# Joining small TensorE steps of a hybrid attention and scan layer: the sample chunk, the outputs of two query blocks, and the form of the first logits

## The chip, the cores and the metric

The kernel runs on one core of a Trainium2 chip. The metric is the device time in microseconds; of several runs the median counts. Time before: 1369.97 us, median of 3 runs (1369.65 to 1371.65).

## What is computed

One layer of a streaming encoder for two request groups that share the weights: a prompt of 512 tokens and a sample of 32 tokens. From the reference, cut to what matters here:

```python
h = rmsnorm(x, g_mix)
q, k, v, z, xbc, dt_raw, gates = split(h @ w_in)
# A: attention; 16 heads of 64; the prompt is causal in chunks of 64 over its 512 tokens,
#    the sample attends to 256 cached rows and its own 32
logits = einsum('bihd,bjhd->bhij', q, k) * HEAD_DIM_A ** -0.5
ya = einsum('bhij,bjhd->bihd', softmax(logits + bias), v)
# B: Mamba-2 scan; 4 groups of 8 heads, chunked over the tokens
y = einsum('bijg,bijgr,bjgrp->bigrp', cb, decay, dx)
y = y + einsum('bign,bgrpn->bigrp', cc, hc) * exp(acs)[..., None]
h_new = hc * exp(last)[..., None, None] + einsum('bjgn,bjgrp->bgrpn', bc, wj)
x = x + (gate_a * (ya @ w_proj_a) + gate_b * (yb @ w_proj_b)) @ w_out
x = x + (gelu(ug) * uv) @ w_down          # ug, uv: causal convolution of rmsnorm(x) @ w_up
x = x + sigmoid(rmsnorm(x) @ w_ple_gate) * (p @ w_ple)
```

## The kernel before

Activations lie with features on partitions and all 544 tokens (512 of the prompt, 32 of the sample) on the free axis. Every dense product is cut into steps of 128 output features, and a step into chunks of 128 input features. A chunk (`Dense.chunk`, L310) is six matmuls `dps` (`mm3`, L273): weight and activation are split into a high and a low fp32r part, three products of them are summed, each for two halves of 272 tokens. One flat list of steps (`dense_steps`, L38) gives the order, and `dense.run(n)` issues the next n chunks. Each weight block is split by ACT (`wh`, L250) and by DVE or POOL (`wl`, L254) ahead of its step.

The scan and the attention are written by hand between those chunks, so that dense matmuls fill the time in which DVE, ACT and POOL prepare the next small matmuls. The order on TensorE is fixed as the program issues it (`Ordered`, L122): every matmul hangs on the one before. The order on the other engines and on SP, which issues the DMAs, is planned by the framework from a simulated timeline.

**Scan** (L1133 to L1147). 20 steps, four groups of 8 heads by five chunks: the sample (`c == 4`, 32 tokens), then prompt chunks 0 to 3 of 128. `ssd_a` (L613) makes the operands of a chunk: `cbt` and `xst` on TensorE, `dx`, `wj` and `bt`, and for each half of 4 heads a tile `ab` (a DMA that broadcasts a row to all partitions) and a tile `m` (Relu head by head, Exp, a mask). `ssd_b` (L661) comes one step later: for each pair of heads the matmuls `yps` from `m` and `dx`, then, in chunks with a state before them, `yps` from `ab` and the state `h`; DVE adds four slices of the result to `xs` (L682); a matmul `st` makes the new state. A step runs 7 chunks between `ssd_a` and `ssd_b` of the chunk before, and 6 behind it: 65 a group. The tiles `dx`, `wj`, `ab`, `m` share 14 buffers (`half_tile`, L607), `bt` has 2, the PSUM tiles of all small matmuls share 4 (`sps`, L172).

**Attention** (L1149 to L1174). Eight pairs of heads, each with four query blocks of 128 (`i` = 0 to 3); pairs with an even number begin with a block for the sample of two pairs (`i` = -1). For a block, `att_a` (L828) makes the logits `L` of both heads and their softmax `P`; one block later `att_b` (L862) transposes `P` (`Tp`) and ACT copies it to `PT`; after some chunks `att_c` (L884) multiplies with the values into `O`, and ACT copies `O` to `att`. `FILL` (L1149) says how many chunks stand before `att_b` and before `att_c`. Blocks 1 to 3 use a stacked form of fp32r operands, made by `stack` (L811) for each head (`hi`) of a pair: `ks` is the high part of k, which a DMA copies to the other 64 partitions; `qs` holds the high part of q on 64 partitions and its low part on the others, for tokens 128 to 511; `klz` is the low part of k. Block 0 takes `q` and `k` as they are, on 64 partitions, in fp32. `stack(m + 1, 0)` is called behind block 3's logits of pair m, `stack(m, 1)` behind block 0's. Each of these tiles has one buffer per head.

A matmul of fp32 operands appears as two instructions in the trace, one of fp32r as one.

Of the kernel before, what the change touches and what calls it, by code (L numbers as in the profile page):

```python
# [9 lines left out]
F32 = mybir.dt.float32  # L10
# [6 lines left out]
SEQ = 512  # L17
SMP = 32
# [98 lines left out]
def trunk(ctx: ExitStack, tc: tile.TileContext, a):  # L117
# [495 lines left out]
    def ssd_a(g, c):  # L613
# [26 lines left out]
        sts = [(bt[:Q], wj.rearrange("p a b -> p (a b)")[:Q])]  # L640
        ms, cps = [], []
        for hh in range(2):
            ab = half_tile("ab")
            src = asc[c, 8 * g + 4 * hh : 8 * g + 4 * hh + 4, 0:Q]
            nc.sync.dma_start(ab[:, :, :Q], src.unsqueeze(0).to_broadcast([128, 4, Q]))
            m = half_tile("m")
            for i in range(4):
                hd = 8 * g + 4 * hh + i
                S.activation(m[:Q, i, :Q], ab[:Q, i, :Q], AF.Relu, scale=-1.0, bias=tm[:Q, 1, c, hd : hd + 1])  # L649
            S.activation(m[:Q, :, :Q], m[:Q, :, :Q], AF.Exp, scale=-1.0)  # L650
            V.tensor_tensor(m[:Q, :, :Q], m[:Q, :, :Q],
                            cbm[:Q, :Q].unsqueeze(1).to_broadcast([Q, 4, Q]), op=MUL)
            ms.append(m)
            if inter:
                S.activation(ab[:, :, :Q], ab[:, :, :Q], AF.Exp)  # L655
                G.tensor_tensor(ab[:, :, :Q], ab[:, :, :Q],  # L656
                                cc[:, tk].unsqueeze(1).to_broadcast([128, 4, Q]), op=MUL)
                cps.append(ab)
        return dxf, sts, ms, cps

    def ssd_b(g, c, dxf, sts, ms, cps):  # L661
        q0 = 128 * c
        Q = 128 if c < 4 else SMP
        tk = slice(q0, q0 + Q)
        inter = c != 0
        hst = state[g, "s"] if c == 4 else state.get(g)
        yp = sps("yps")
        for pr in range(4):
            for hi in range(2):
                hd = 2 * pr + hi  # L670
                PE.matmul(yp[64 * hi : 64 * hi + 64, 128 * pr : 128 * pr + Q],
                          lhsT=dxf[:Q, 64 * hd : 64 * hd + 64], rhs=ms[hd // 4][:Q, hd % 4, :Q],
                          start=True, stop=not inter)
            if inter:
                for hi in range(2):
                    hd = 2 * pr + hi
                    PE.matmul(yp[64 * hi : 64 * hi + 64, 128 * pr : 128 * pr + Q],
                              lhsT=hst[:, 64 * hd : 64 * hd + 64], rhs=cps[hd // 4][:, hd % 4, :Q],
                              start=False, stop=True)
        for i in range(4):  # L680
            t = xs[4 * g + i]
            V.scalar_tensor_tensor(t[:, tk], t[:, tk], vec[:, V_DSK + 4 * g + i : V_DSK + 4 * g + i + 1],  # L682
                                   yp[:, 128 * i : 128 * i + Q], op0=MUL, op1=ADD)
        st = sps("st")
        for n, (l, r) in enumerate(sts):
            PE.matmul(st, lhsT=l, rhs=r, start=True, stop=True)
        hn = spt([128, 512], "h", 4)
        if inter:
            G.tensor_tensor(hn.rearrange("p (h f) -> p h f", f=64), hst.rearrange("p (h f) -> p h f", f=64),
                            el[:, c, 8 * g : 8 * g + 8].unsqueeze(2).to_broadcast([128, 8, 64]), op=MUL)  # L690
            V.tensor_tensor(hn, hn, st, op=ADD)
        else:
            S.copy(hn, st)
        if c == 4:
            nc.sync.dma_start(a["o_hs"][:, 512 * g : 512 * g + 512], hn)
        else:
            state[g] = hn
            ssd_done.add((g, c))
            if c == 3:
                nc.sync.dma_start(a["o_hp"][:, 512 * g : 512 * g + 512], hn)  # L700
# [110 lines left out]
    def stack(m, hi):  # L811
        q, k = qk["q", m], qk["k", m]

        def st(n, tag):
            return pools["ap"].tile([128, n], F32R, tag=tag, name=tag, bufs=1)

        kl = klz[hi]
        a0, b0 = 64 * hi, 64 - 64 * hi
        own, oth = slice(a0, a0 + 64), slice(b0, b0 + 64)
        qs, ks = st(384, f"qs{hi}"), st(512, f"ks{hi}")  # L820
        S.copy(ks[own], k[own, 0:512])
        nc.sync.dma_start(ks[oth].bitcast(F32), ks[own].bitcast(F32))
        S.copy(qs[own], q[own, 128:512])
        V.tensor_tensor(qs[oth], q[own, 128:512], qs[own].bitcast(F32), op=SUB)  # L824
        G.tensor_tensor(kl[own], k[own, 0:512], ks[own].bitcast(F32), op=SUB)
        stk[hi] = qs, ks, kl

    def att_a(m, i):  # L828
# [15 lines left out]
        for hi in range(2):  # L844
            p0 = 64 * hi
            L = sps("L")
            own = slice(p0, p0 + 64)
            if i == 0:
                PE.matmul(L[:, :n], lhsT=q[own, 0:n], rhs=k[own, 0:n], start=True, stop=True)
            else:  # L850
                qs, ks, kl = stk[hi]
                sl = slice(n - 256, n - 128)
                PE.matmul(L[:, :n], lhsT=qs[:, sl], rhs=ks[:, 0:n], start=True, stop=False)
                PE.matmul(L[:, :n], lhsT=qs[:, sl], rhs=kl[:, 0:n], start=False, stop=True)
# [7 lines left out]
    def att_b(m, i, Ps):  # L862
# [12 lines left out]
        for hi in range(2):  # L875
# [3 lines left out]
            pt = apt([128, 512], "PT", 2)  # L879
# [4 lines left out]
    def att_c(m, i, pts):  # L884
        O = sps("O")
        if i < 0:
            pt = pts[0]
            for w in range(2):
                cv, vs = qk["cv", m + w], qk["s", m + w]
                for j in range(3):  # L890
                    for hi in range(2):
                        p0 = 64 * hi
                        lhs = cv[:, j, p0 : p0 + 64] if j < 2 else vs[:, p0 : p0 + 64]
                        kk = 128 if j < 2 else SMP
                        o = 128 * j + 64 * w + 32 * hi
                        PE.matmul(O[p0 : p0 + 64, SMP * w : SMP * w + SMP], lhsT=lhs, rhs=pt[:kk, o : o + 32],
                                  start=j == 0, stop=j == 2)
            for w in range(2):
                if m + w not in att:
                    att[m + w] = slot(name="at", src=at_slots)  # L900
                S.copy(att[m + w][:, SEQ:T], O[:, SMP * w : SMP * w + SMP])
            return
        at, vt = att[m], qk["v", m]
        n = 128 * (i + 1)
        for j in range(i + 1):
            for hi in range(2):
                p0 = 64 * hi
                PE.matmul(O[p0 : p0 + 64, 0:128], lhsT=vt[:, 128 * j + p0 : 128 * j + p0 + 64],
                          rhs=pts[hi][:, 128 * j : 128 * j + 128], start=j == 0, stop=j == i)
        S.copy(at[:, 128 * i : n], O[:, 0:128])  # L910
# [235 lines left out]
    ssd_b(*prev)  # L1146
# [123 lines left out]
```

## Time and profile before

| | before |
|---|---|
| median of 3 runs | 1369.97 us |
| the profiled execution, time | 1369.19 us |
| its span | 1367.5 us |
| TensorE busy (matmuls) | 99% |
| DVE, ACT, POOL busy | 62%, 47%, 23% |

The span is what the profile covers; the time of the same execution has 1.7 us around it. A busy share of TensorE is not its pace: matmuls overlap in the records, so a matmul's length in a row is longer than its share of the time, and the pace is the distance between the starts of successive rows. In a timeline row the first number is the start, the second the length of the merged row, then engine, line, operation, output <- inputs, the tile shape of the array that the matmul uses (rows \* columns), the moving operand's shape, and xN for N instructions in the row.

### The profile page before, as it was taken

To read this page: it belongs to the slowest core of one execution; us is meant where nothing else is said; L and a number is where in the kernel's file an instruction comes from. 1 tells how busy PE (TensorE), PEld (TensorE's weight loads), DVE (VectorE), ACT (ScalarE), POOL (GpSimd) and SP (SyncE) were. 2 spreads that over 40 slices of the span, in tenths; PEclk is the share of its full clock that TensorE was granted. 3 is DMA by queue.
4 is the path that set the end of the run, shared out by engine and by line. 5 is a ranking of instruction groups with operands and counts; after the bars stand their busy time and mean duration, and the time that the engine had idled before them with its cause. 6 is when DMAs were issued, how large, how long until landed. Compare 5 with 4: busy or idle time off the path is not lost.

```text
span 1367.5 us, 26629 instructions
## 1 busy us (share of the span) xinstructions
PE 1350.5 (99%) x11045; PEld 1311.3 (96%) x11045; DVE 848.5 (62%) x1474; ACT 643.3 (47%) x1156; POOL 318.2 (23%) x446
## 2 busy tenths in 40 slices
PE   7999999999999999999999999999999999999998
PEld 6999999999899999999999999999999999999998
DVE  7998878855676555752545335677777447753545
ACT  5456565656576666652433223444444224431342
POOL 5446364543331111200000000033333013310000
PEclk9999999999999999999999999999999999999999
DMA  5733232433434323212222332222222232222231
GB/s 180 249 105 105 101 119 96 137 99 127 151 100 135 116 88 103 70 63 93 93 93 82 129 104 93 93 93 81 78 91 93 93 110 81 77 95 93 93 104 55
DMA packets 41961, 142.16 MB, mean 104 GB/s; under 512 B 9280, under 2 KB 13296, under 8 KB 29552
## 3 DMA queue, kind: packets, MB, share of 16 engines
q1 hardware_dynamic: 41840, 140.46, 30.9%
q8 instruction: 87, 1.43, 0.4%
q14 instruction: 34, 0.28, 0.1%
HBM read 129.27 MB, written 14.31 MB: 105 GB/s over the span
## 4 chain that ended last, share of the span: by engine, by line
PE 96%; DVE 1%; ACT 1%; DMA 0%; issue 0%; SPq 0%; DVEq 0%; ACTq 0%
PE dps L130 84%; PE yps L130 3%; PE O L130 2%; PE L L130 2%; PE st L130 2%; PE Tp L133 1%; PE xst L133 1%; DVE qs L824 1%; PE qn L130 0%; PE gps L130 0%; DMA xin<-in_xT 0%; PE cbt L130 0%; PE vt L133 0%; ACT wh L250 0%; ACT P L777 0%
## 5 line engine op out<-in xcount | busy, mean ns | idle before, releaser
L130 PE MATMUL dps<-hi,wh 128*128 128x272 f32 x2960 | 629.0, 294 | 1.2 <-ACT hi L374 0.5
L130 PE MATMUL dps<-lo,wh 128*128 128x272 f32 x2960 | 614.1, 289 | 5.6 <-DVE lo L375 5.6
L130 PE MATMUL dps<-hi,wl 128*128 128x272 f32 x2960 | 613.2, 289 | 0.0
L130 PEld LDWEIGHTS dps<-hi,wh 128*128 128x128 f32 x2960 | 466.9, 189 | 15.6 <-issue 10.9
L130 PEld LDWEIGHTS dps<-lo,wh 128*128 128x128 f32 x2960 | 466.8, 189 | 6.6 <-DVE lo L375 6.6
L130 PEld LDWEIGHTS dps<-hi,wl 128*128 128x128 f32 x2960 | 466.3, 189 | 0.0
L250 ACT CAST wh<-wr 128x1024 fp32r<-128x1024 f32 x192 | 201.4, 1049 | 395.3 <-PE dps L130 355.9
L254 DVE TENSOR_TENSOR wl<-wr,wh 128x1024 fp32r<-128x1024 f32 x173 | 214.6, 1240 | 49.2 <-ACT wh L250 43.8
L1026 DVE SCALAR_TENSOR_TENSOR ucv<-uext,vec,ucv 128x546 f32<-128x546 f32 x96 | 75.3, 785 | 4.1 <-ACT ucv L1023 2.4
L599 DVE SCALAR_TENSOR_TENSOR cv<-ext,hv,cv 128x547 f32<-128x547 f32 x72 | 68.7, 954 | 5.8 <-ACT cv L596 5.0
L1019 POOL COPY cfo<-uext 128x2 f32<-128x2 f32 x48 | 10.4, 217 | 260.4 <-DVE uext L573 260.4
L1016 POOL MEMSET uext<- 128x2 f32 x48 | 4.5, 94 | 278.3 <-issue 278.3
L1058 DVE TENSOR_TENSOR x<-x,dps 128x544 f32<-128x544 f32 x24 | 17.3, 721 | 78.0 <-PE dps L130 78.0
L254 POOL TENSOR_TENSOR wl<-wr,wh 128x1024 fp32r<-128x1024 f32 x19 | 47.5, 2500 | 58.4 <-ACT wh L250 58.4
L571 DVE TENSOR_TENSOR uext<-dps,rstd 128x272 f32<-128x272 f32 x48 | 21.2, 441 | 63.7 <-PE dps L130 59.0
L775 DVE CUSTOM_DVE_ANT_0 P<-L,bias 128x128 f32<-128x128 f32 (+3 forms) x64 | 30.9, 482 | 46.8 <-PE L L130 46.8
L1020 POOL COPY cfo<-uext 128x2 f32<-128x2 f32 x48 | 56.4, 1175 | 0.0
L649 ACT ACTIVATE m<-ab,tm 128x128 f32<-128x128 f32 (+1 forms) x160 | 48.3, 374 | 4.9 <-DMA ab<-asc 4.9
L777 ACT ACTIVATE P<-P,sm 128x128 f32<-128x128 f32 (+3 forms) x64 | 35.9, 561 | 23.7 <-DVE sm L775 23.5
L656 POOL TENSOR_TENSOR ab<-ab,bc 128x512 f32<-128x512 f32 (+1 forms) x32 | 40.2, 1262 | 28.7 <-ACT ab L655 28.6
L368 ACT CAST hi<-me 128x544 fp32r<-128x544 f32 x24 | 15.5, 647 | 61.9 <-DVE me L1044 61.9
L731 POOL TENSOR_TENSOR ql<-qs,qh 128x544 fp32r<-128x544 f32 x16 | 22.5, 1405 | 94.3 <-ACT qh L730 81.5
(240 smaller groups left out, 1564.5 us busy)
## 6 DMA issues: line engine op xcount, KB each, us to landing
wr<-in_w SPq DMA_DIRECT2D x96, 1024.0 KB, 4.9
ab<-asc SPq DMA_DIRECT2D x32, 256.0 KB, 5.1
bsc<-evec SPq DMA_DIRECT2D x16, 320.0 KB, 7.5
bias<-bsc SPq DMA_DIRECT2D x16, 256.0 KB, 3.6
xin<-in_xT SPq DMA_DIRECT2D x8, 272.0 KB, 5.1
out_o_v<-v SPq DMA_DIRECT2D x8, 272.0 KB, 2.5
out_o_k<-qk SPq DMA_DIRECT2D x8, 272.0 KB, 2.1
x<-in_xT SPq DMA_DIRECT2D x8, 272.0 KB, 4.4
```

The lines of the kernel that those rows point to most:

```text
L130: return self._pin(nc.tensor.matmul(*args, **kw))
L133: return self._pin(nc.tensor.transpose(*args, **kw))
L250: cp = S.copy(hi, r)
L254: eng.tensor_tensor(lo, r, hi.bitcast(F32), op=SUB)
L599: V.scalar_tensor_tensor(y[:, :n], ext[:, j : j + n], hv[:, 24 * j + ti : 24 * j + ti + 1], y[:, :n], op0=MUL, op1=ADD)
L649: S.activation(m[:Q, i, :Q], ab[:Q, i, :Q], AF.Relu, scale=-1.0, bias=tm[:Q, 1, c, hd : hd + 1])
L656: G.tensor_tensor(ab[:, :, :Q], ab[:, :, :Q], cc[:, tk].unsqueeze(1).to_broadcast([128, 4, Q]), op=MUL)
L731: G.tensor_tensor(lo[:, :T], sq[:, :T], hi[:, :T].bitcast(F32), op=SUB)
L775: V.tensor_tensor_reduce(out=P, in0=L, in1=B, scale=1.0, scalar=3e38, op0=ADD, op1=MIN, accum_out=nm[:n])
L777: S.activation(P, P, AF.Exp, scale=-1.0, bias=nm[:n], accum_out=sm[:n])
L1020: G.tensor_copy(cfo[:, i, 2:4], ext[:, UW - 2 : UW])
L1026: V.scalar_tensor_tensor(y[:, :n], ext[:, j : j + n], vec[:, V_FW + 48 * j + i : V_FW + 48 * j + i + 1], y[:, :n], op0=MUL, op1=ADD)
```

## The change

Four things are rearranged. (1) The sample chunk of a group has no step of its own: `ssd_a` for it and for chunk 0 stand together, and `ssd_b` takes both as one list: all `yps` of the sample (16 instructions from `m` and `dx`, then 16 from `ab` and `h`), then chunk 0's, then DVE's additions, then both `st`. The sample's eight heads lie in one `ab` and one `m`, with one DMA, one subtraction on DVE and one Relu on ACT in place of eight. 16 steps remain, with 65 chunks a group as before. (2) `att_c` takes two blocks at one place (0 and 1 with the sample, if there is one; 2 and 3), with one `O` and one copy for both. (3) Block 0 uses the stacked form too: `qs` covers all 512 tokens, and both heads are stacked behind block 3's logits of the pair before. (4) `PT` of even blocks has two buffers of its own.

```diff
@@ ssd_a
-        for hh in range(2):
-            ab = half_tile("ab")
-            src = asc[c, 8 * g + 4 * hh : 8 * g + 4 * hh + 4, 0:Q]
-            nc.sync.dma_start(ab[:, :, :Q], src.unsqueeze(0).to_broadcast([128, 4, Q]))
...
+        H = 4 if c < 4 else 8
+        for h0 in range(0, 8, H):
+            ab = half_tile("ab").rearrange("p a b -> p (a b)")[:, 0 : H * Q].rearrange("p (h q) -> p h q", q=Q)
+            src = asc[c, 8 * g + h0 : 8 * g + h0 + H, 0:Q]
+            nc.sync.dma_start(ab, src.unsqueeze(0).to_broadcast([128, H, Q]))
...
+            else:
+                V.tensor_tensor(m, ab[:Q], tm[:Q, 1, c, 8 * g : 8 * g + 8].unsqueeze(2).to_broadcast([Q, H, Q]),
+                                op=SUB)
+                S.activation(m, m, AF.Relu, scale=-1.0)
...
@@ ssd_b
+    def ssd_b(parts):
+        yps = []
+        for g, c, dxf, bt, wj, ms, cps in parts:
...
+            for hds in ([range(8)] if c == 4 else [range(h, h + 2) for h in range(0, 8, 2)]):
+                heads(dxf, Q, ms, True, c == 0)
+                if c != 0:
+                    heads(hst, 128, cps, False, True)
+        for (g, c, *_), yp in zip(parts, yps):
...
+                V.scalar_tensor_tensor(x_[:, tk], x_[:, tk], vec[:, V_DSK + 4 * g + i : V_DSK + 4 * g + i + 1],
+                                       yp[:, 128 * i : 128 * i + Q], op0=MUL, op1=ADD)
+        for g, c, dxf, bt, wj, ms, cps in parts:
...
+            PE.matmul(st, lhsT=bt[:Q], rhs=wj.rearrange("p a b -> p (a b)")[:Q], start=True, stop=True)
...
@@ stack
-        qs, ks = st(384, f"qs{hi}"), st(512, f"ks{hi}")
+        qs, ks = st(512, f"qs{hi}"), st(512, f"ks{hi}")
...
-        S.copy(qs[own], q[own, 128:512])
-        V.tensor_tensor(qs[oth], q[own, 128:512], qs[own].bitcast(F32), op=SUB)
+        S.copy(qs[own], q[own, 0:512])
+        V.tensor_tensor(qs[oth], q[own, 0:512], qs[own].bitcast(F32), op=SUB)
@@ att_a
-            if i == 0:
-                PE.matmul(L[:, :n], lhsT=q[own, 0:n], rhs=k[own, 0:n], start=True, stop=True)
-            else:
...
+            qs, ks, kl = stk[hi]
+            PE.matmul(L[:, :n], lhsT=qs[:, n - 128 : n], rhs=ks[:, 0:n], start=True, stop=False)
+            PE.matmul(L[:, :n], lhsT=qs[:, n - 128 : n], rhs=kl[:, 0:n], start=False, stop=True)
@@ att_b
-            pt = apt([128, 512], "PT", 2)
+            pt = apt([128, 512], "PT", 2) if i % 2 else apt([128, 384], "PTe", 2)
@@ att_c
-    def att_c(m, i, pts):
+    def att_c(parts):
         O = sps("O")
...
+        m, i, _ = parts[-1]
+        S.copy(att[m][:, 128 * i - 128 : 128 * i + 128], O[:, 0:256])
...
@@ the loops
-    for n in range(20):
-        g, c = n // 5, (4, 0, 1, 2, 3)[n % 5]
-        nxt = (g, c) + ssd_a(g, c)
-        dense.run(7)
+    for n in range(16):
+        g, c = divmod(n, 4)
+        nxt = [ssd_a(g, i) for i in ((4, 0), (1,), (2,), (3,))[c]]
+        fa, fb = ((10, 9), (8, 8), (8, 7), (8, 7))[c]
+        dense.run(fa)
         if prev is not None:
-            ssd_b(*prev)
+            ssd_b(prev)
         prev = nxt
-        dense.run(6)
-        if n == 14:
+        dense.run(fb)
+        if n == 11:
...
     stack(0, 0)
+    stack(0, 1)
...
             if st[1] == 3 and st[0] + 1 < NPAIR:
                 stack(st[0] + 1, 0)
-            elif st[1] == 0:
-                stack(st[0], 1)
+                stack(st[0] + 1, 1)
...
-            att_c(prev[0], prev[1], pts)
+            cs.append((prev[0], prev[1], pts))
+            if prev[1] in (1, 3):
+                att_c(cs)
+                cs = []
```

## Rows read from the trace of the kernel before

**Rows 1.** The page's first part: busy us, share of span, instructions, by engine.
```profile
PE 1350.5 (99%) x11045; PEld 1311.3 (96%) x11045; DVE 848.5 (62%) x1474; ACT 643.3 (47%) x1156; POOL 318.2 (23%) x446
```

**Rows 2.** The chain that ended last, in order of time: start, us, what.
```profile
872.77 444.26 PE dps L130 x3534
```

**Rows 3.** Waits of TensorE: who waited for whom, us in total, times, longest.
```profile
PE st L130 <- DVE xs L682: 2.6, 2, 1.3
PE O L130 <- ACT PT L880: 1.3, 3, 0.4
```

**Rows 4.** Timeline of TensorE in the scan, group 0: sample, then chunk 0.
```profile
91.28 0.42 PE L130 MATMUL dps<-hi,wl 128*128 128x272 f32 x2
91.62 0.30 PE L130 MATMUL yps<-m,dx 32*64 32x32 f32 x4
...
93.51 1.12 PE L130 MATMUL st<-wj,bt 32*128 32x512 f32 x2
...
94.92 0.41 PE L130 MATMUL dps<-lo,wh 128*128 128x272 f32 x2
...
105.34 1.09 PE L130 MATMUL yps<-m,dx 128*64 128x128 f32 x16
106.36 1.12 PE L130 MATMUL st<-wj,bt 128*128 128x512 f32 x2
...
107.57 0.41 PE L130 MATMUL dps<-lo,wh 128*128 128x272 f32 x2
```

**Rows 5.** Timeline of TensorE in attention, pairs 0 and 1.
```profile
363.88 0.49 PE L130 MATMUL L<-qk 64*128 64x128 f32 x4
...
372.59 0.41 PE L130 MATMUL dps<-hi,wl 128*128 128x272 f32 x2
372.93 0.44 PE L130 MATMUL O<-PT,vt 128*64 128x128 f32 x4
373.30 0.44 PE L130 MATMUL L<-ks,qs 128*128 128x384 f32 x1
373.58 0.33 PE L130 MATMUL L<-klz,qs 128*128 128x384 f32 x1
373.75 0.34 PE L130 MATMUL L<-ks,qs 128*128 128x384 f32 x1
...
383.77 0.88 PE L130 MATMUL O<-PT,vt 128*64 128x128 f32 x12
384.58 0.49 PE L130 MATMUL L<-qk 64*128 64x128 f32 x4
385.00 0.52 PE L130 MATMUL dps<-hi,wh 128*128 128x272 f32 x2
385.35 0.41 PE L130 MATMUL dps<-lo,wh 128*128 128x272 f32 x2
```

**Rows 6.** Timeline of TensorE, the sample's outputs in attention.
```profile
367.85 0.42 PE L130 MATMUL O<-pts,cv 128*64 128x32 f32 x8
368.20 0.30 PE L130 MATMUL O<-pts,vs 32*64 32x32 f32 x4
```

**Rows 7.** One line's instructions (L824): count, ns min/median/max, first and last start, shapes.
```profile
L824 DVE TENSOR_TENSOR qs<-qk,qs x16: 552/1333/1544, 355.7 to 559.4; 64x384 fp32r<-64x384 f32 x16
```

**Rows 8.** Timeline of DVE, pair 6, block 3: the second `P`.
```profile
565.18 0.48 DVE L779 TENSOR_SCALAR P<-P,sm 128x512 f32<-128x512 f32 x1
```

**Rows 9.** Timeline of TensorE, pair 6, block 3: the transposes of both `P`.
```profile
565.52 1.03 PE L133 MATMUL Tp<-ident,P 128*128 128x128 f32 x8
```

**Rows 10.** Timeline of SP's queue at the start of attention.
```profile
359.81 1.14 SPq L822 DMA_DIRECT2D ks<-ks x2
```

**Rows 11.** The line of that DMA, 353 to 366 us: issue to landing.
```profile
DMA to landing us min/median/max: 3.5/3.5/3.6
```

**Rows 12.** Busy time by stretch: stretch, length, engines, granted clock, DMA share, GB/s.
```profile
161.60:164.80 3.20, 3.20 (x15) 3.20 (x15) 2.71 (x8) 3.14 (x9) 0.00 (x0) 0.50 0.00 0
```

**Rows 13.** Waits of all engines.
```profile
ACT bt L629 <- DVE cbt L627: 20.4, 12, 3.2
```

More of the change, by code (lines that the diff above doesn't have):

```diff
@@ L659, in ssd_a @@
[L659 to L691, printed above, removed]
-        else:
[L693 to L700, printed above, removed]
@@ new lines, in ssd_a, with heads @@
+        return g, c, dxf, bt, wj, ms, cps
+    def ssd_b(parts):
+        yps = []
+        for g, c, dxf, bt, wj, ms, cps in parts:
+            Q = 128 if c < 4 else SMP
+            hst = state[g, "s"] if c == 4 else state.get(g)
+            yp = sps("yps")
+            yps.append(yp)
+            def heads(lhs, k, rhs, first, last):
+                for hd in hds:
+                    start = first and (c < 4 or hd < 2)
+                    stop = last and (c < 4 or hd >= 6)
+                    p0 = 64 * (hd % 2)
+                    PE.matmul(yp[p0 : p0 + 64, 128 * (hd // 2) : 128 * (hd // 2) + Q],
+                              lhsT=lhs[:k, 64 * hd : 64 * hd + 64], rhs=rhs[hd], start=start, stop=stop)
+            for hds in ([range(8)] if c == 4 else [range(h, h + 2) for h in range(0, 8, 2)]):
[3 more added lines that the diff above has]
+        for (g, c, *_), yp in zip(parts, yps):
+            q0 = 128 * c
+            Q = 128 if c < 4 else SMP
+            tk = slice(q0, q0 + Q)
+            for i in range(4):
+                x_ = xs[4 * g + i]
+                V.scalar_tensor_tensor(x_[:, tk], x_[:, tk], vec[:, V_DSK + 4 * g + i : V_DSK + 4 * g + i + 1],
+                                       yp[:, 128 * i : 128 * i + Q], op0=MUL, op1=ADD)
+        for g, c, dxf, bt, wj, ms, cps in parts:
+            Q = 128 if c < 4 else SMP
+            hst = state[g, "s"] if c == 4 else state.get(g)
+            st = sps("st")
+            PE.matmul(st, lhsT=bt[:Q], rhs=wj.rearrange("p a b -> p (a b)")[:Q], start=True, stop=True)
+            hn = spt([128, 512], "h", 4)
+            if c != 0:
+                G.tensor_tensor(hn.rearrange("p (h f) -> p h f", f=64), hst.rearrange("p (h f) -> p h f", f=64),
+                                el[:, c, 8 * g : 8 * g + 8].unsqueeze(2).to_broadcast([128, 8, 64]), op=MUL)
+                V.tensor_tensor(hn, hn, st, op=ADD)
+            else:
+                S.copy(hn, st)
+            if c == 4:
+                nc.sync.dma_start(a["o_hs"][:, 512 * g : 512 * g + 512], hn)
+            else:
+                state[g] = hn
+                ssd_done.add((g, c))
+                if c == 3:
+                    nc.sync.dma_start(a["o_hp"][:, 512 * g : 512 * g + 512], hn)
@@ L900, in att_c @@
                     att[m + w] = slot(name="at", src=at_slots)
[L901 to L910, printed above, removed]
+                S.copy(att[m + w][:, SEQ:T], O[:, 256 + SMP * w : 256 + SMP * w + SMP])
         if i == 3:
```

69 lines of the change are left out of this document (36 added, 33 removed).

## The prediction, made before the result was known

> **What bounds the kernel now.** I read the busy shares of the page first: TensorE stands at 99% of a span of 1367.5 us [rows 1]. Since matmuls overlap, I then read the chain of work in order of time. From 872.77 us on it is one run of 3534 matmuls `dps` in 444.26 us, 0.1257 us each [rows 2], with nothing between: from about 601 us to the end TensorE runs at its pace, and nothing in the change touches that stage. Third, the waits of TensorE: they are few, 1.3 us in `O` and 2.6 us in `st` [rows 3]. So the stages that the change touches (the scan, 86 to 352 us, and attention, 352 to 601 us) are bound by TensorE too, and what counts is the time from the start of one group of matmuls to the start of the next in its timeline. The reader should see there that small groups pay a fixed price at both ends. A pair of `dps` matmuls takes 0.25 us, but 0.34 when `yps` or `O` follows (91.28 to 91.62, 372.59 to 372.93) [rows 4, 5], and the first matmul after such a group is late too (0.28 against 0.17 for `L`) [rows 5]. The tile shape in the row changes at each of these places, from 128\*128 to 128\*64, 32\*64 or 64\*128.
>
> **The change, part by part.** The number of dense chunks is the same (65 for each scan group, and the same fill in attention), so those cancel.
>
> *Sample chunk joined with chunk 0, four groups.* Before, the sample's `ssd_b` is 0.09 late start, 1.89 of `yps` (91.62 to 93.51), and `st` with the next pair 1.41, less that pair's 0.25: 3.14 us. Chunk 0 is 0.09, 1.02, and 1.21 less 0.25: 2.07 us. Together 5.21 [rows 4]. The sample's `yps` costs more than chunk 0's although its matmuls have 32 columns and not 128: it goes through eight groups of four instructions, 0.236 us each, whose shape alternates between 32\*64 and 128\*64. The change issues all 16 instructions of one shape, then all 16 of the other. What a longer group costs is shown by the sample's `O`: eight instructions 128\*64 with 32 columns take 0.35 us [rows 6], so four more cost 0.115, and 16 cost 0.236 + 3 x 0.115 = 0.58. Twice that is 1.16. Then chunk 0's `yps` 1.02, the sample's `st` 1.05 (between 0.96 and 1.16, since another `st` follows), chunk 0's `st` 0.96, start 0.09: 4.28 us. Gain 0.93 a group, **3.7 us**; bounds 0.4 (only the late start saved) and 4.8. The two `ssd_a` stand together as well and save about one late start, 0.09 each: **0.4 us** (0 to 0.8).
>
> By the Trainium skill ("TensorE: Matmul & The Clock Gate", LDWEIGHTS (loading the stationary operand)) a weight load takes its columns divided by 1.2 in ns, here 53 ns for 64 columns, whatever the rows. Were that the pace, the 32 instructions would take 1.71 us and not 1.16 (an estimate from that page). The trace does not agree: eight such instructions in 0.35 us [rows 6] are 44 ns each, a change of shape included.
>
> *Attention outputs of two blocks at one place.* A block's `O` takes 0.37 us for 4 instructions and 0.81 for 12 [rows 5]: 0.22 for each four and 0.15 fixed. With 0.09 before it and 0.11 after it (0.28 less 0.17), a place costs 0.35. There were 36 places (four in each of eight pairs, and four samples), now 16: 16 merges of prompt blocks save 0.35 each, and four sample merges 0.20 each, since the sample ends in another shape and keeps its fixed part: 5.6 + 0.8 = **6.4 us** (4.0 if only both ends are saved, 7.0 if all is). The Trainium skill says the same of the cause ("TensorEngine Tiling (Array Packing)", Key Properties: a change of tiling mode drains the engine).
>
> *First logits in the 128-row form.* Before: 0.42 us in 64\*128 (384.58 to 385.00) and the next pair 0.35 and not 0.25 [rows 5], 0.52. After: four matmuls of 128 columns in 128\*128. No row has that form; those of 384 columns take 0.17 [rows 5], a third of it is 0.06, and I take 0.10, between these: 0.40. In the four odd pairs the place was behind an `O` that now goes away, and its share of the 0.11 counted above is not there, so I count 0.52 - 0.40 = 0.12 less 0.11; in the three later even pairs it follows an `O` still, 0.52 against 0.51; at pair 0 it saves 0.22. Sum **0.3 us** (a gain of 1.6 at 0.06, a loss of 2 at 0.17).
>
> *Waits taken away.* `O` waited for ACT's `PT` three times, 1.3 us [rows 3]; these are the `O` of block 2 in odd pairs, which now stand behind block 3. **1.3 us** (0 to 1.3).
>
> *Waits added by the stacks.* Both halves' `ks`, `qs`, `kl` must now be there for block 0, not block 1. They can't be made earlier than block 3's logits of the pair before, whose tiles they overwrite. Both halves are made together already, ahead of block 0's logits, where the tiles allow it: their DMAs stand side by side [rows 10]. `qs` has 512 columns and not 384: 0.552 us where it runs alone, up to 1.544 behind POOL's `klz` [rows 7]; the shortest, scaled, gives 0.18 more a stack. Queued behind them on DVE is the softmax of block 3. Where its cover is thin: at pair 6 the second `P` is ready at 565.66 (565.18 + 0.48) [rows 8], while its transposes start at 565.52 [rows 9]. TensorE now comes 1.0 us earlier (the `O` and the logits in front of it), four transposes pass first (about 0.4), and DVE is up to 0.36 later: about 1.1 us. At the start, the two DMAs of `ks` are issued from 359.81 to 360.95 [rows 10] and take 3.5 us [rows 11], against block 0's logits at 363.88 [rows 5]: 0.5 us (0 to 3.5, one landing). I add 0.4 for the other pairs. Sum **+2.0 us** (0 to 8, one for each pair).
>
> *Waits added in the scan.* The pool for `bt` has two buffers. The joined step holds two, so chunk 1's copy, and chunk 0's in groups 1 to 3, waits for an `st` of the step before, and with it a PSUM tile `cbt` stays. Then four tiles carry `cbt`, two `yps`, two `st`: the second `st` needs DVE's four `xs` on the first `yps`. The nearest row is the same wait, 1.3 us at most [rows 3]; cover is chunk 0's `yps` and the first `st`, 2.07 us. I take **+1.0 us** (0 to 5.2, four times 1.3). ACT does fewer activations for the sample, DVE one subtraction more, SP four DMAs fewer; beside TensorE all of that is hidden, and if DVE's cover is gone it is the wait just priced.
>
> *Clock.* After the sample of groups 1 and 2 the granted clock fell to half (0.50, so 1.2 GHz) for about 3 us (the row is group 1's) [rows 12], at a cost of half of that, 1.6 us; after groups 0 and 3 it did not. I leave the two as they are (0 to 4 times: -3.2 to +3.2).
>
> **Sum.** -3.7 - 0.4 - 6.4 - 0.3 - 1.3 + 2.0 + 1.0 = -9.1 us. The profiled execution took 1369.19 us, so 1360.1; the median of the runs is 0.78 higher, so **1360.9 us**.
>
> **The rivals.**
> *The fixed price belongs to each block, not to the place.* Then merging saves the two ends alone (4.0 and not 6.4 us) and the sample's `yps` stays at 1.89 (2.9 us less): 1360.9 + 2.4 + 2.9 = 1366.2. For it: all rows have one block to a place. Against: 0.236 for four and 0.35 for eight of the same form [rows 4, 6]. Chance 0.10.
> *Weight loads set the pace of the sample.* Chunk 0's `yps` has the same 64 weight columns and takes 1.02 us for 16 [rows 4]; at that pace the sample's 32 need 2.04, so nothing is gained on today's 1.89 and 0.73 is lost in four groups: 1363.8. Against: the 44 ns of [rows 6]. Chance 0.05. The rule of the Trainium skill above would do this; by its figure the time is 1363.1.
> *The stacks come late.* One us in each pair and 2 at the start, 10 us for the 2.0 counted: 1368.9. For: `qs` and `klz` lengthen each other, and DVE also carries the softmax. Against: at the passages into even pairs the sample's block stands between, and the row of pair 6 is the thinnest cover that I found. Chance 0.12. This is also how the change could fail to do what it says.
> *ACT stands at `bt`: slower.* ACT already waits 20.4 us in front of `bt`, 12 times, 3.2 at the longest [rows 13]. With two buffers for three steps its copy hangs on a matmul `st` that comes 8 to 10 chunks later; what is queued behind it on ACT are the casts `wh` of the next weights. If the copy stands early in ACT's queue, TensorE runs out of weights, at seven places (chunk 1 in four groups, chunk 0 in three). At 3.2 us each, 22 us for the 1.0 counted: 1382; it turns the sign from 1.4 us a place. Against: ACT's order is planned, and a cast is due only every eight chunks. Chance 0.08.
> *More goes away.* Both clock drops (3.2 us) and the `st` waits (2.6): 1355.1. Chance 0.10.
>
> **How the numbers follow.** Forecast 0.55, with its own range 1356 to 1365. The range 1354 to 1368.5 takes in the first two rivals, the last and a part of the stacks; it leaves out the slow one and extremes. A measurement of this kernel tells about 0.2%, 2.7 us: faster means under 1367.2, slower over 1372.7. Faster: 0.55 + 0.10 + 0.05 + 0.10 and 0.03 of the stacks, 0.83. Same: 0.08 of the stacks, 0.01 of `bt`, 0.09. Slower: 0.07 of `bt` and 0.01 of the stacks, 0.08.
>
> **What would show it.** In the changed kernel's timeline: the sample's `yps` as two groups of 16 that start about 0.58 us apart; one `O` place in two blocks, with 0.15 + 0.22 for each four; block 0's `L` at about 0.10 each in 128\*128. Among the waits: none of `O` for `PT` in odd pairs, one of the transposes for DVE's `P` at pair 6, `st` for `xs` at most 1.3. The stage from the end of attention to the end must keep its length. I am wrong if the two groups of `yps` together stay near 1.9 us, if TensorE waits for `ks` or `qs` in most pairs, or if `dps` waits for `wh` in the scan.

## The result, and the profile after

The changed kernel takes 1356.34 us (median of 4 runs, 1355.65 to 1357.59) against 1369.81 for the kernel before (4 runs): a ratio of 0.9906, 95% interval 0.9893 to 0.9920. The forecast was 1360.9 with a range of 1354.0 to 1368.5. The sign, the range and most steps held; the gain is 13.5 us where 9.1 were worked out. The forecast misses by 4.6 us: the granted clock, the waits of the scan and the start of the scan came out better than worked out, the stacks worse. The parts below take this apart. The profiled execution took 1355.77 us, its span is 1354.1.

The busy shares of the changed kernel, as in [rows 1], and the last piece of its chain, as in [rows 2]:

```profile
PE 1338.2 (99%) x11045; PEld 1307.2 (97%) x11045; DVE 852.6 (63%) x1474; ACT 634.4 (47%) x1104; POOL 313.7 (23%) x442
```

```profile
859.45 444.25 PE dps L130 x3534
```

TensorE is still busy 99% of the span, and the last stage has its length to 0.01 us. It only starts 13.3 us earlier. The waits of TensorE (who waited for whom, us in total, times, longest) answer to [rows 3]:

```profile
PE st L130 <- DVE xs L690: 1.8, 2, 1.2
...
PE L L130 <- DMA ks<-ks: 1.0, 2, 0.8
PE Ls L130 <- DVE qk L756: 0.9, 3, 0.3
PE L L130 <- ACT qs L752: 0.6, 1, 0.6
PE Tp L133 <- DVE sm L788: 0.5, 1, 0.5
PE st L130 <- DVE m L656: 0.3, 1, 0.3
```

`O` no longer waits for `PT`. In its place stand four small rows in attention (`L`; `Ls`, the sample's logits; `Tp`, the transposes of `P`), 3.0 us in all. The timeline of TensorE in the scan, group 1, shows the joined step (in [rows 4] the sample's eight alternating groups run from 91.62 to 93.51):

```profile
162.41 0.65 PE L130 MATMUL yps<-m,dx 32*64 32x32 f32 x16
163.00 0.66 PE L130 MATMUL yps<-ab,h 128*64 128x32 f32 x16
163.48 1.07 PE L130 MATMUL yps<-m,dx 128*64 128x128 f32 x16
164.49 2.18 PE L130 MATMUL st<-wj,bt 32*128 32x512 f32 x4
...
166.75 0.41 PE L130 MATMUL dps<-lo,wh 128*128 128x272 f32 x2
```

The sample's 32 instructions take 0.59 + 0.48 = 1.07 us (1.89 before). The timeline of attention, pair 1 (two blocks at one `O` place) and the logits of block 0 in pair 2:

```profile
379.90 0.88 PE L130 MATMUL O<-PTe,vt 128*64 128x128 f32 x12
380.61 1.04 PE L130 MATMUL O<-PT,vt 128*64 128x128 f32 x16
381.58 0.39 PE L130 MATMUL L<-ks,qs 128*128 128x256 f32 x1
...
410.46 0.33 PE L130 MATMUL L<-ks,qs 128*128 128x128 f32 x1
410.63 0.28 PE L130 MATMUL L<-klz,qs 128*128 128x128 f32 x1
410.74 0.27 PE L130 MATMUL L<-ks,qs 128*128 128x128 f32 x1
410.85 0.28 PE L130 MATMUL L<-klz,qs 128*128 128x128 f32 x1
```

28 instructions of `O` take 1.68 us from the first start to the start of `L`, and block 0's logits start 0.11 us apart (0.17 for the first, which stands behind `O`).

For the comparison of runs, the span is cut where four rows of TensorE's timeline start: the first `cbt` of the scan, the last `st`, the last `O` and the last `gps`, a small matmul near the end. "Falls" are stretches of about 3 us in the scan in which the granted clock is half and the `dps` pairs start 0.45 and not 0.25 us apart; one of e4's three is twice as long.

| kernel (profiled execution) | start of scan | scan | attention | rest | falls |
|---|---|---|---|---|---|
| before | 74.95 | 276.70 | 248.35 | 762.47 | 2 |
| after | 73.10 | 268.97 | 244.68 | 762.41 | 0 |
| e1 before again | 75.13 | 276.74 | 248.34 | 762.47 | 2 |
| e2 scan part only | 75.95 | 269.05 | 248.26 | 762.46 | 0 |
| e3 outputs only | 74.86 | 276.72 | 240.55 | 762.41 | 2 |
| e4 first logits only | 73.06 | 279.79 | 246.92 | 762.47 | 3 |
| e5 after again | 75.62 | 270.63 | 243.61 | 762.37 | 1 |
| e6 joined, alternating | 73.88 | 270.00 | 243.68 | 762.41 | 0 |
| e7 without first logits | 76.30 | 268.84 | 240.60 | 762.40 | 0 |
| e8 stacks given more time | 73.28 | 268.93 | 241.29 | 762.40 | 0 |
| e9 e7, the two `st` apart | 74.44 | 267.78 | 240.62 | 762.40 | 0 |
| e10 grouped, not joined | 73.42 | 270.81 | 248.32 | 762.46 | 0 |
| e11 e10 again | 74.50 | 270.80 | 248.35 | 762.47 | 0 |
| e12 a chunk between | 75.88 | 277.52 | 248.29 | 762.46 | 2 |

The start moves by up to 3.2 us between kernels that are equal up to there, and by 2.5 between two executions of the changed one (73.10, 75.62). So 1.85 us of the 13.4 by which the two spans differ belong to no part of the change. Two things differ there between the two traces: the granted clock is 0.50 from 14.65 to 21.48 us in the kernel before and from 16.51 to 19.92 us in the changed one, and TensorE waits 5.6 and 4.1 us for `lo`, an operand that DVE makes; they were not taken apart. The scan gives 7.7, attention 3.7.

### The profile page after: what moved, and what is told of

Same layout as the page of the kernel before. It is cut to its first block, busy times and chain, and to the rows that moved or that the text cites. A ratio compares the mean times of both kernels' runs of the same rounds, so it can differ in the third digit from the quotient of the medians.

```text
span 1354.1 us, 26563 instructions
## 1 busy us (share of the span) xinstructions
PE 1338.2 (99%) x11045; PEld 1307.2 (97%) x11045; DVE 852.6 (63%) x1474; ACT 634.4 (47%) x1104; POOL 313.7 (23%) x442
## 4 chain that ended last, share of the span: by engine, by line
PE 89%; DVE 6%; ACT 2%; DMA 1%; issue 1%; SPq 0%; POOL 0%; ACTq 0%; DVEq 0%; POOLq 0%
PE dps L130 80%; PE O L130 2%; PE yps L130 2%; PE L L130 1%; PE st L130 1%; DVE cv L599 1%; DVE qs L834 1%; PE Tp L133 1%; DVE wl L254 1%; PE xst L133 0%; PE gps L130 0%; DMA wr<-in_w 0%; DVE xs L603 0%; DMA ab<-asc 0%; PE qn L130 0%
## 5 line engine op out<-in xcount | busy, mean ns | idle before, releaser
L660 POOL TENSOR_TENSOR ab<-ab,bc 128x512 f32<-128x512 f32 (+1 forms) x28 | 37.0, 1325 | 40.7 <-ACT ab L659 40.7
L1030 ACT ACTIVATE ucv<-uext,vec 128x546 f32<-128x546 f32 x48 | 40.7, 847 | 7.2 <-DVE uext L574 2.6
L650 ACT ACTIVATE m<-ab,tm 128x128 f32<-128x128 f32 x128 | 40.8, 389 | 6.3 <-DMA ab<-asc 6.2
```

Source lines behind the costliest of these rows:

```text
L650: S.activation(m[:, i], ab[:Q, i], AF.Relu, scale=-1.0, bias=tm[:Q, 1, c, hd : hd + 1])
L660: G.tensor_tensor(ab, ab, cc[:, tk].unsqueeze(1).to_broadcast([128, H, Q]), op=MUL)
L1030: S.activation(y[:, :n], ext[:, 0:n], AF.Identity, scale=vec[:, V_FW + i : V_FW + i + 1], bias=vec[:, V_FB + i : V_FB + i + 1])
```

## The experiments

**Is the difference the kernel's or the execution's?** e1 is the kernel before and e5 the changed kernel, both unaltered.

> The kernel before, unchanged, for a second trace of it: it tells how much of the difference between the two traces (13.4 us of span) is one execution against another. Theory: the start (1.85 us, the first scan matmul at 74.95 us before and 73.10 after) and the two falls of the granted clock behind the sample (3 us together) belong to single executions, so this trace may show the start up to 2 us elsewhere and 0 to 4 falls. Rival: both belong to the kernel, then the first scan matmul stands at 74.9 +- 0.3 and the same two falls are there.

Measured: 1369.42 us. The rival held: scan and attention repeat to 0.04 us, the start is 75.13 (74.95 before), and the two falls stand behind the sample of the same two groups (the slow pairs begin at 162.3 and 231.0 us).

> The changed kernel once more, for a second trace and as the measure of the next ones. Theory: stage lengths repeat to 0.3 us (scan 269.0, attention 244.7, the rest 762.4), the start is within 1.5 us of 74.5, no fall of the clock behind the joined sample. Rival (the falls are chance): one to three falls in the scan, which is then 1.5 to 4.5 us longer.

Measured: 1356.96 us, ratio 0.9916 (0.9897 to 0.9934). The stages did not repeat to 0.3 us. One fall appeared, from about 235 us, behind a wait of 1.2 us of `st` for `xs`, and the scan is 1.66 us longer for it; the first execution has a wait of that length at the same `st` and no fall. Attention is 243.61, 1.07 us shorter than in the first execution. The stretch (us, busy us of PE, PEld, DVE, ACT, POOL, granted clock, DMA share, GB/s):

```profile
236.50:239.50 3.00, 3.00 (x15) 2.48 (x15) 3.00 (x7) 0.82 (x3) 2.70 (x2) 0.64 0.11 35
```

The last part of this stretch is at full clock again. So a fall costs about 1.6 us and isn't impossible in the new kernel.

**Each part alone.** e2 makes only the scan part (both diffs of `ssd_a` and `ssd_b`, the loop over 16 steps), e3 only the outputs (`att_c(parts)` and `PTe`), e4 only the first logits:

```diff
e3, on the kernel before
-            att_c(prev[0], prev[1], pts)
+            cs.append((prev[0], prev[1], pts))
+            if prev[1] in (1, 3):
+                att_c(cs)
+                cs = []
e4, on the kernel before
-        qs, ks = st(384, f"qs{hi}"), st(512, f"ks{hi}")
+        qs, ks = st(512, f"qs{hi}"), st(512, f"ks{hi}")
...
-            elif st[1] == 0:
-                stack(st[0], 1)
+                stack(st[0] + 1, 1)
```

> Only the joined sample step of the scan, attention as before. Theory (the fixed price of a change of shape, 1.0 us in each of four groups, and falls of the clock that the shorter sample passage avoids): 1369.8 - 4.1 - 3 - about 1 of st waits, 1361 to 1364, scan from its first to its last matmul 268 to 271 us where before it is 276.7. Rival (the order of the other engines made the scan shorter, the joining itself gives nothing): 1367 to 1370, scan 275 to 277 us.

Measured: 1360.87 us, 0.9947 (0.9932 to 0.9962). The scan is 269.05 long, as the theory expected, no falls, `st` waits for `xs` 1.9 us. The whole gain of the scan, 7.7 us, comes from this part.

> Only the outputs of two blocks at one place and the buffers of PT that this needs; scan and first logits as before. Theory (20 places fewer at 0.35 or 0.2 us, and the waits of O for PT gone): 1369.8 - 6.4 - 1.3 to 1.9 = 1361.5 to 1362.5. Rival (the fixed price belongs to each block, not to the place): 1369.8 - 4.0 = 1365.8. A second rival, that TensorE's earlier arrival is given back in waits for the softmax: over 1366.

Measured: 1360.56 us, 0.9940 (0.9922 to 0.9958). Attention is 240.55 long: 7.8 us saved, for 6.4 + 1.3 worked out. Neither `O` nor `L` nor `Tp` is among its waits (`lo`, `warm`, `hi` and `ext` belong to the time before the scan):

```profile
PE dps L130 <- DVE lo L375: 5.7, 3, 2.8
PE st L130 <- DVE xs L682: 2.6, 2, 1.3
PE warm L130 <- DVE wz L221: 1.3, 1, 1.3
PE dps L130 <- ACT hi L374: 0.5, 1, 0.5
PE dps L130 <- DVE ext L574: 0.4, 1, 0.4
```

> Only block 0's logits in the stacked form, with both stacks behind block 3 of the pair before. Theory (the form gives nothing on TensorE, four matmuls of 0.11 to 0.13 us for 0.52 before, and the earlier due time of the stacks brings waits of 2 to 4 us): 1370 to 1374. Rival (the form itself is worth its place): 1367 to 1369.

Measured: 1367.99 us, 1.0001 (0.9991 to 1.0011). Attention is 1.4 us shorter, about what the waits of `O` for `PT` were (1.3), and `L` waits 0.3 for `ks`. The theory's 1370 to 1374 failed, and the time lies in the rival's range without a gain to show for the form: in the profiled execution the scan, which this part doesn't touch, has three falls, one twice as long, and is 3.1 us longer. The ten runs have a mean granted clock of 0.992 to 0.996, the 13 of the kernel before beside them 0.995 to 0.997. The last two results together are the clue. The 1.4 are the same waits that e3 takes away, so both parts together should still give about 7.8; they give 3.7. Something costs some 4 us only where both are there.

**The first logits taken back out.** e7 is the changed kernel with `stack` and block 0's logits as before (e4's diff reversed). e8 keeps the changed kernel and moves two chunks in even pairs from behind block 3's transposes to behind block 2's, which puts more dense work between block 3's logits, behind which the stacks are made, and the next block 0:

```diff
e8, on the changed kernel
-    FILL = {(0, -1): (2, 2), (0, 0): (3, 1), (0, 1): (1, 3), (0, 2): (2, 3), (0, 3): (2, 4),
+    FILL = {(0, -1): (2, 2), (0, 0): (3, 1), (0, 1): (1, 3), (0, 2): (2, 5), (0, 3): (2, 2),
```

> The changed kernel without its third part: block 0's logits in the old form, second stack behind block 0. Theory (the third part alone gives nothing that counts, and together with the merged outputs it costs 4.1 us of waits, since the O in front of block 0 is gone and the stacks have less time): attention 240.5 and not 244.7, scan 269.0, 1352 +- 1.5. Rival (parts add up as each alone against the kernel before: -7.7, -7.8, -1.4): the third part is worth 1.4 us here too, 1357.5 to 1358.

Measured: 1352.26 us, 0.9879 (0.9859 to 0.9898). Attention is 240.60, the same as in e3. Without its third part attention is 4.1 us shorter than in the changed kernel's first execution, 3.0 than in e5's.

> The changed kernel with two chunks of fill moved from behind block 3's transposes in even pairs to ahead of the next pair's block 0, so that its logits come 1.5 us later. Theory (the stacks' tiles and DMAs are late): the waits and stretched starts of L at the passages into odd pairs, 2.3 us in the trace of the changed kernel, fall under 0.5, attention 242.4 to 243.2; O of block 3 may wait for PT up to 0.3 in four pairs instead. Rival (a PSUM tile is missing, not an operand): the waits of L stay, attention 244.5 to 245.

Measured: 1352.54 us in a single run; attention 241.29, shorter than either theory had it. All waits of `L` and `Tp` are gone, only `Ls` keeps its 0.9:

```profile
PE st L130 <- DVE xs L690: 1.8, 2, 1.1
...
PE Ls L130 <- DVE qk L756: 0.9, 3, 0.3
```

So the cost of the third part is lateness, not the form of the logits. With the form kept and the stacks given time, 3.4 of the 4.1 us come back (2.3 of 3.0 against e5's execution). What was late can be read in the changed kernel around 426 to 432 us, before block 0 of pair 3. DVE:

```profile
425.56 0.69 DVE L785 CUSTOM_DVE_ANT_0 P<-L,bias 128x512 f32<-128x512 f32 x1 [1.85 <-PE L L130]
...
426.51 3.06 DVE L834 TENSOR_TENSOR qs<-qk,qs 64x512 fp32r<-64x512 f32 x2 [0.25 <-ACT qs L833]
...
429.69 0.67 DVE L785 CUSTOM_DVE_ANT_0 P<-L,bias 128x512 f32<-128x512 f32 x1
```

ACT in the same stretch:

```profile
425.33 0.62 ACT L831 CAST ks<-qk 64x512 fp32r<-64x512 f32 x1
425.85 0.62 ACT L833 CAST qs<-qk 64x512 fp32r<-64x512 f32 x1
426.50 0.62 ACT L831 CAST ks<-qk 64x512 fp32r<-64x512 f32 x1
427.03 0.61 ACT L833 CAST qs<-qk 64x512 fp32r<-64x512 f32 x1
...
431.12 0.47 ACT L752 ACTIVATE qs<-qn,eps 128x272 f32<-128x272 f32 x1
```

SP's queue, the two `ks` DMAs, and their time from issue to landing (view of the tile, 421 to 433 us):

```profile
426.02 0.47 SPq L832 DMA_DIRECT2D ks<-ks  x1
...
427.22 0.47 SPq L832 DMA_DIRECT2D ks<-ks  x1
```

```profile
DMA to landing us min/median/max: 4.3/4.3/4.4
```

TensorE, block 0's logits:

```profile
430.76 0.22 PE L130 MATMUL L<-ks,qs 128*128 128x128 f32 x1
...
431.70 0.30 PE L130 MATMUL L<-ks,qs 128*128 128x128 f32 x1 [0.60 <-ACT qs L752]
```

The two `qs` of the stacks stand on DVE between the two softmax halves of block 3 and hold the second for 3.1 us; at pair 6 the two are part of the DVE work in front of the late transpose. Four casts hold ACT for 2.3, and the second head's `ks` is cast behind both casts of the first: its DMA is issued 1.2 us after the first, at 427.22, and lands 4.3 to 4.4 us later, at about 431.6. The second `L` starts at 431.70. The row puts its wait down to ACT's read of `qn` (L752), which ends at 431.59, almost together with the landing. The second execution of the same kernel, e5, tells the two apart. Its ACT, its TensorE, and its chain of work in the same place:

```profile
434.89 0.47 ACT L752 ACTIVATE qs<-qn,eps 128x272 f32<-128x272 f32 x1
```

```profile
435.32 0.30 PE L130 MATMUL L<-ks,qs 128*128 128x128 f32 x1 [0.45 <-DMA ks<-ks]
```

```profile
431.00 4.19 DMA ks<-ks
435.18 0.14 issue
```

There `L` starts before ACT's read has ended (435.36), and again 0.14 us behind the landing. So what is late is the copy of `ks`. It is the same at pair 5, where the second `L` stands 0.81 us for it:

```profile
490.51 0.30 PE L130 MATMUL L<-ks,qs 128*128 128x128 f32 x1 [0.81 <-DMA ks<-ks]
```

The two `ks` DMAs of that pair, from the view of the tile between 470 and 495 us, and all 16 of the kernel, from the view of line L832:

```profile
DMA to landing us min/median/max: 5.0/5.0/5.0
```

```profile
DMA to landing us min/median/max: 2.2/3.3/5.0
```

At pair 5 they need 5.0 us from issue to landing, where 3.5 had been read at the start of attention [rows 11]. In e7 the two `qs` stand between the same two halves on DVE (2.89 us from 428.69), but block 0's logits take `q` and `k` as they are and need neither `qs` nor `ks`.

**The scan: the order of the sample's matmuls.** e6 is the changed kernel with the sample's shapes alternating again. e10 is the kernel before with only that order changed: own step as before, the sample's 16 and 16 instructions grouped; e11 is the same again.

```diff
e6, on the changed kernel
-            for hds in ([range(8)] if c == 4 else [range(h, h + 2) for h in range(0, 8, 2)]):
+            for hds in ([range(h, h + 2) for h in range(0, 8, 2)]):
e10 and e11, on the kernel before
+        if c == 4:
+            for lhs, k, rhs, first in ((dxf, Q, ms, True), (hst, 128, cps, False)):
+                for hd in range(8):
+                    p0 = 64 * (hd % 2)
+                    PE.matmul(yp[p0 : p0 + 64, 128 * (hd // 2) : 128 * (hd // 2) + Q],
+                              lhsT=lhs[:k, 64 * hd : 64 * hd + 64], rhs=rhs[hd // 4][:k, hd % 4, :Q],
+                              start=first and hd < 2, stop=not first and hd >= 6)
```

> The changed kernel, with the sample's yps again in pairs that alternate between the two shapes; joined step, one ab and m and all else stay. Theory (the change of shape is the price): yps of the sample 1.9 us and not 1.07 in each of four groups, scan 269.0 + 3.3 = 272.3, and if the long passage of alternating small matmuls is what lets the clock fall, 1.5 us more for each fall, up to four: 1359 to 1364. Rival (the gain comes from the joining and the fewer instructions on the other engines): scan 269.0 to 269.5, no fall, 1356 +- 1.

Measured: 1357.24 us, 0.9917 (0.9899 to 0.9936), no different from the changed kernel. The expectation of the theory failed, and the rival's scan (269.0 to 269.5) was not met either: it is 270.00. The price of the shape is there: the sample's `yps` takes 1.79 us (96.59 to 98.38) where the changed kernel needs 1.07, 2.9 us in four groups:

```profile
96.59 0.30 PE L130 MATMUL yps<-m,dx 32*64 32x32 f32 x4
96.83 0.31 PE L130 MATMUL yps<-ab,h 128*64 128x32 f32 x4
...
98.24 0.31 PE L130 MATMUL yps<-ab,h 128*64 128x32 f32 x4
98.38 1.07 PE L130 MATMUL yps<-m,dx 128*64 128x128 f32 x16
```

But the waits of `st` for `xs` (1.8 us) are gone: TensorE comes 0.7 us later to the same place, and at the longer of the two waits DVE was also sooner done with the work in front of `xs` (two `cv` took 1.60 us from 227.40, and 3.58 from 226.79 in the changed kernel). So the scan is only 1.03 us longer. A gain in front of a wait can be paid back at the wait.

> The kernel before, with only the order of the sample's yps changed (16 of one shape, then 16 of the other); the sample keeps its own step. Theory (a change of shape costs about 0.12 us): yps of the sample 1.1 us and not 1.89, 3.1 us less in four groups if no wait takes it back; and if the length of the sample's passage is what lets the clock fall, at most one fall in four groups: scan 270.5 to 272, 1362 to 1364. Rival (the falls hang on the sample's own step, st behind yps with dense work around it): two falls or more, scan 273 to 274, 1364.5 to 1366.

Measured: 1362.32 us, 0.9958 (0.9941 to 0.9974). The theory held. The scan is 5.9 us shorter, without falls: `yps` is 1.18, so 0.71 in each of four groups is 2.8, and the two missing falls are 3.1.

```profile
90.09 0.65 PE L130 MATMUL yps<-m,dx 32*64 32x32 f32 x16
90.68 0.66 PE L130 MATMUL yps<-ab,h 128*64 128x32 f32 x16
91.27 1.12 PE L130 MATMUL st<-wj,bt 32*128 32x512 f32 x2
```

> The same kernel as the run before, for a second trace and four more passages of the sample. The first theory expects at most one fall of the clock, the rival two or more, as for that run.

Measured: 1362.83 us, scan 270.80, no falls. Three quarters of what the scan gained in these traces, the two falls among it, come with the order of 32 instructions; joining the sample with chunk 0 adds 1.8.

**What the falls hang on.** e12 leaves the sample's step of the kernel before as it is and only puts a dense chunk between its `yps` and its `st`:

```diff
e12, on the kernel before
+        if c == 4:
+            dense.run(1)
         st = sps("st")
...
-        dense.run(6)
+        dense.run(5 if c == 0 else 6)
```

> The kernel before, with one dense chunk (six matmuls dps) between the sample's yps and its st, taken from the six behind the step; the eight alternating groups of yps stay as they are (1.89 us). Theory: the falls of the granted clock hang on the unbroken passage of small matmuls, yps and st together (about 3.1 us); the chunk breaks it, at the price of one more change of shape (0.1 to 0.2 us in each of four groups), so the falls vanish (none in the four groups), the scan is 276.7 - 2 x 1.55 + 0.6 = 274.2 us long, and the time is about 1367. Rival: the alternation of the shapes is what brings them, and they stay: about two falls in four groups, the scan 276.8 to 278.5, the time 1369 to 1371. The waits of st for xs are 2.6 in the kernel before, none of them at a sample's st, and stay in both cases.

Measured: 1368.46 us, 0.9998 (0.9980 to 1.0017). The theory failed and the rival held: two falls in four groups, scan 277.52. Group 1, the passage and then the fall (columns as above; the clock is the number behind POOL's):

```profile
160.00:163.70 3.70, 3.70 (x39) 2.50 (x37) 3.67 (x7) 3.02 (x7) 0.00 (x0) 1.00 0.47 166
163.70:166.90 3.20, 3.20 (x15) 3.20 (x16) 2.42 (x7) 2.48 (x7) 0.00 (x0) 0.52 0.18 67
```

**A better version.** e9 is e7 with two chunks between the sample's `st` and chunk 0's, so that DVE can finish its additions before the second `st` needs its PSUM tile:

```diff
e9, on e7
             if c == 4:
                 nc.sync.dma_start(a["o_hs"][:, 512 * g : 512 * g + 512], hn)
+                dense.run(2)
...
-        fa, fb = ((10, 9), (8, 8), (8, 7), (8, 7))[c]
+        fa, fb = ((10, 9), (8, 6), (8, 7), (8, 7))[c]
```

> The kernel without the third part, with two of the dense chunks that stood behind the joined step now between the sample's st and chunk 0's st. Theory (chunk 0's st waits for the PSUM tile that DVE's xs frees; 1.5 us of dense work covers it): the waits of st for xs, 1.7 us in two groups, are gone, scan 267.0 to 267.5 and not 268.8, 1350.5 +- 1.5. Rival (the dense work between brings a price of its own at each place, or the wait moves to the next tile): scan 268.5 to 269.5, 1352 +- 1.5.

Measured: 1350.71 us, 0.9871 (0.9857 to 0.9886), the lowest median of this study, 5.6 us under the changed kernel's; in time its interval overlaps e7's. The scan is 267.78, between what the theory and the rival expected: the wait for `xs` fell from 1.7 to 0.3 us, and the scan gained 1.06 of these 1.4. That the extra changes of shape around the chunks kept the rest is likely, but was not measured.

```profile
PE st L130 <- DVE xs L690: 0.3, 1, 0.3
```

## Why the prediction was right, and where it was not

**Bound.** Right: TensorE's pace sets the time in all stages; the stage behind attention kept its length (762.47 and 762.41 us).

**The joined sample step (3.7 + 0.4).** Right in size and mechanism. The passage was to take 4.28 us for the 5.21 before; it takes 0.09 + 2.08 (162.41 to 164.49) + 2.01 (164.49 to 166.75, less a `dps` pair's 0.25) = 4.18. That is 1.03 a group, 4.1 in four, for the 3.7; group 1 has no wait in this passage. The sample's `yps` was put at 1.16 and is 1.07. The 0.4 of the two `ssd_a` was not measured by itself.

**The outputs (6.4 + 1.3).** Right. The price, 0.15 and 0.22 for each four, gives 1.69 us for 28 instructions and 0.81 for 12; the rows have 1.68 and 0.81 (394.65 to 395.46). e3 shows 7.8 us for the sum of 7.7, with the waits of `O` gone as worked out. The Trainium skill ("TensorEngine Tiling (Array Packing)", Key Properties) names the cause that was drawn on, a drain at each change of tiling mode. It gives no price; the traces put one at 0.24 us for a group of four with its change, against 0.12 for four more of the same shape.

**First logits (0.3) and the stacks (+2.0).** The logits came out about as worked out: a matmul of the new form starts 0.11 to 0.13 us after the one before, for 0.10 taken, and attention in e8, less its 0.9 us of `Ls`, is 0.2 us shorter than in e7 with the old form (an estimate from two single traces). Of the stacks the kind of loss was right, the size was not. The passage of pair 6 was named, and it came as described, 0.45 us for the 1.1 worked out. In the timeline of the transposes:

```profile
552.67 0.63 PE L133 MATMUL Tp<-ident,P 128*128 128x128 f32 x4 [0.45 <-DVE sm L788]
```

But 0.4 us was added for all other pairs, and they cost most: between e7 and the changed kernel lie 4.1 us (3.0 for e5's execution), where the two terms together made 1.7. The rows of waits name 3.0 of these 4.1; e8 shows that 3.4 hang on when the stacks are due. Another 0.7 stay, the 0.9 of `Ls`, which waits for `qk` on DVE, less the 0.2 above; why `qk` is late was not followed. The step that failed is "I add 0.4 for the other pairs": pair 6 was taken as the thinnest place after looking at the softmax alone, and the landing of `ks` was followed only at the start of attention. At pairs 3 and 5 the second `ks` is issued 1.2 us after the first, behind ACT's casts, and needs 4.2 to 5.0 us to land in the two executions, and the second `L` waits 0.4 to 0.8 us for it each time. The rival "the stacks come late" had this mechanism at 10 us; 3 to 4 of those 10 came. At the start of attention, for which 0.5 was counted, no wait is listed, but the second `L` starts 0.32 us (354.27 to 354.59) and not 0.11 behind the matmul before it, so about 0.2 came.

**Waits added in the scan (+1.0).** The wrong way round. `st` waits for `xs` at the new place, 1.2 us at the longest, within the bound of 1.3 a group. But the 2.6 us of before were left standing in the sum. They are two waits in group 3 (at 313.75 and 343.71 us), which stay in e10; with the sample joined only the 0.3 for `m` is left in that group, and why was not followed. Together 2.1 us now (1.8 for `xs`, 0.3 for `m`) against 2.6, a gain of 0.5 for a loss of 1.0. ACT's stand at `bt`, the slower rival, didn't come: no `dps` of the scan waits for `wh`.

**Clock (0).** Wrong. The two falls were left as they are, and both went, worth 3.1 us (e10: scan 5.9 shorter, of which `yps` 2.8). That part of "more goes away" is what happened. The prediction had the row [rows 12] and noted that the falls follow a sample step, but named no cause and left their number open. The counts in the last section, e10's and e12's above all, tie them to a step of the sample's own with alternating shapes; which trait of that step counts isn't shown.

**The other rivals.** "Price per block" wanted `yps` at 1.89 and "weight loads set the pace" wanted 2.04 us for the sample's 32; both fall with 1.07 (at 2.04 the second would have come to 1364.4, not to 1363.8). By the rule of the Trainium skill cited in the prediction ("TensorE: Matmul & The Clock Gate", LDWEIGHTS (loading the stationary operand)) 16 loads of 64 columns would take 0.85 us (an estimate from that page); the second group of 16 took 0.48, so the trace goes on disagreeing.

**The sum again.** From 1369.19 to 1355.77 are 13.4 us. The 9.1 worked out, 3.1 of the clock, 1.5 of the waits in the scan and 1.85 of an earlier start, less 2.4 for the stacks, make 13.15. So the forecast is near by luck in part: the start belongs to no part of the change, and the falls and the stacks were both missed and partly cancel.

## What to carry to other kernels

Count the changes of a matmul's tile shape, not the matmuls: put all instructions of one shape together, and independent blocks at one place, and each change avoided gave about 0.12 us here, where TensorE was bound and no wait behind it took the gain back, as one did between e6 and the changed kernel. When a change makes TensorE arrive earlier, follow every producer of the next place (each engine's queue, the PSUM tile, the landing of every DMA and not of the first alone) and not the one that looks thinnest: two parts that are each worth something alone can take from each other. If a producer must be ready one block earlier, give it that time by moving dense work ahead of the place, as e8 did, or leave its consumer as it was, as e7 did.

## What the hardware showed that was not expected

**The granted clock falls without an idle TensorE.** In e12 it is 1.00 over the passage and 0.52 over the next 3.2 us (1.2 GHz for nearly all of that), TensorE busy in all of both. Counted over the profiled executions, a separate sample step with alternating shapes (before, e1, e3, e4, e12) has 11 falls in 20 groups; the same step grouped (e10, e11) none in 8; the step joined with chunk 0 and grouped (after, e2, e5, e7, e8, e9) one in 24, and that one stands behind a wait of 1.2 us, which the first execution has without a fall. The runs as a whole agree: the mean granted clock, which takes in the start as well, is 0.990 to 0.997 in the 40 runs of the kernel before that were taken beside the experiments, and 0.997 to 0.998 in the five of e10 and e11. The same kernel can show another number of falls the next time, so these are rates of a few executions. In the joined step falls are rarer, not excluded: the changed kernel's slowest run (1357.59 us) has the lowest mean granted clock of its four, 0.995 against 0.997 to 0.999. The Trainium skill ("TensorE: Matmul & The Clock Gate", What's actually happening) ties the half clock to an engine that has been idle, and says that the gate goes by how busy it has been; here the first doesn't hold, and the second isn't tested. What decides stays open: in e6, alternating but followed at once by chunk 0's 16 matmuls of 128 columns, there was no fall in four groups, and a dense chunk in that place (e12) didn't help. Where in time the passage came wasn't varied on its own.

**Two engines at one stack.** DVE's `qs` takes 0.69 us where POOL has nothing to do (the shortest of 16, below) and 1.53 each (3.06 for two, at 426.51) beside POOL's two `klz`. The Trainium skill ("SBUF — State Buffer", SBUF: two separate sides) says that these two engines hold their shared port in turn, for a whole instruction each; the times agree, and the doubled instruction is the one that held block 3's softmax.

```profile
L834 DVE TENSOR_TENSOR qs<-qk,qs x16: 686/1392/1796, 346.2 to 547.3; 64x512 fp32r<-64x512 f32 x16
```
